# A RWKV-7 recurrence beside dense products: TensorE's order written out, preparation two chunks ahead, the inverse by blocks of 16, attention's parities in turn

## The chip, the cores and the metric

The kernel runs on one core of one Trainium2 chip. The metric is the device time of one execution in microseconds (us); the kernel before takes 3066.93 us, the median of three runs. Engines are TensorE (PE: matmuls; its weight loads, PEld, are listed apart), VectorE (DVE), ScalarE (ACT), GpSimd (POOL) and SyncE (SP, which issues the loads and stores).

## The reference

One inference step of a two-layer streaming encoder: 1024 new frames of one stream and 64 frames of another that is running. Width 1024, 16 heads of 64. Layer 0 mixes time by RWKV-7 and has a SwiGLU FFN; layer 1 is sliding-window attention with sinks over a shared key/value projection, and another FFN. All in float32. The recurrence, per head, with a 64×64 state:

```python
def step(s, inp):
    r_t, w_t, k_t, v_t, a_t, b_t = inp
    sa = jnp.einsum('bhvk,bhk->bhv', s, a_t)
    s = s * w_t[:, :, None, :] + sa[..., None] * b_t[:, :, None, :] + v_t[..., None] * k_t[:, :, None, :]
    return s, jnp.einsum('bhvk,bhk->bhv', s, r_t)
```

Its outputs are normalised per head, get a bonus term and a gate, and go through the output projection. Outputs of the whole are both streams' results, the two final states, the shift rows and the new key/value caches.

## The kernel before

**Dense products.** Weights are loaded in rows of 128×512 (`wr`), split into a high part `wh` (L393, ACT) and a remainder `wl` (L394, DVE or POOL); activations likewise into `xh` and `xl`. A product is three matmuls, `wh·xh`, `wh·xl`, `wl·xh` (L433, L434, L435), into a PSUM tile `dp`. Tokens go in two halves: A, of 512 columns (chunks 0 to 7), and B, of 576 (chunks 8 to 15 and the second stream), in pieces of 288 or 290 columns.

**Recurrence.** 17 chunks of 64 tokens: 0 to 7, 8 to 15, and 16, the second stream. A chunk is a few bursts of small matmuls between element-wise work:

- `prep` loads r, k, a and the decay; norms of the keys (`pn`, 8 matmuls, L106 to L117), scaled pairs `AR` and `BK`, the products G = BK·AR (two halves of 8 matmuls, into two banks of tag `rp` each, read out by L152 under a mask), and the bonus (L157, L158).
- `prep2` inverts the 64×64 triangular matrices of the 16 heads (`inverse`) and transposes BK into `BT` (L175 to L177). The inverse solves the four 32×32 diagonal quarters of all heads by substitution on DVE (15 steps, two columns a step, up to two parts each: L215 multiplies, L219 sums), after ACT has copied the triangles into a broadcast layout (L190), and joins quarters by two rounds of 16 matmuls of 32×32 (`r_ixd`, tag `rc`).
- `chain` is what follows from chunk to chunk: `U0` from the state M, `Up` = W·U0, the new state `Sp`, and the output Y of two state reads (even heads, then odd, kept in this order by a small memset `by`, L281) and the rows of G.
- `post` normalises (L318, L322 and L323 on POOL), transposes back (4 matmuls, `c_id` times `r_yc`), applies gate and bonus and stores z.

**Order.** Every instruction carries a priority (`Two`: one for TensorE, another for the rest), and a scheduler orders each engine's queue by it and by when operands will be there. Chunk i+1's `prep` and `prep2` stand behind chunk i's chain. The first eight chunks lie beside half B's decay, rate and gate stages and its v, r and k products; chunks 8 to 16 beside half A's output projection (`mix_out`), its norm, and the FFN of half A. An engine executes its queue in order and waits at an instruction whose semaphores aren't there yet.

**Attention.** For each pair of heads `attend` scales the probabilities, transposes them (`pt`, L1290), copies them out and multiplies by the values (`po`, L1294), first the one parity (partitions 0 to 63 of `po`) and then the other (64 to 127).

Of the kernel before, what the change touches and what calls it, by code (L numbers as in the profile page):

```python
# [9 lines left out]
F32 = mybir.dt.float32  # L10
F32R = mybir.dt.float32r
AF = mybir.ActivationFunctionType
ALU = mybir.AluOpType
# [34 lines left out]

class Rwkv:
# [32 lines left out]
    def start(self):  # L82

        nc = self.nc
        self.W = self.sb.tile([128, 8, 64], F32, name="W", tag="W", bufs=1)
        nc.gpsimd.memset(self.W, 0.0)

    def prep(self, ch):
# [14 lines left out]

        pn = self.pp()[0:64, 0:16].rearrange("p (par j) -> p par j", par=2)
        for j in range(8):
            self.mm(pn[:, :, j], lhsT=sq[:, j, :], rhs=c["bd"][:, 0:128:64], start=True, stop=True)  # L106
        n4 = self.t([128, 32], "n4")
        for q in range(4):
            d = 32 * (q % 2)
            V.tensor_scalar(out=n4[32 * q:32 * q + 32].rearrange("p (g j) -> p g j", g=4),  # L110
                            in0=mid(pn[d:d + 32, q // 2, :], 4), scalar1=1e-24, scalar2=None, op0=ALU.max)
        V.reciprocal(out=n4, in_=n4)
        nl = self.t([128, 32], "nl", 3)
        V.transpose(out=nl, in_=n4)

# [25 lines left out]


        X = self.t([128, 16, 128], "G", 2)
        flat2 = lambda x: x.rearrange("p a b -> p (a b)")
        for g in range(2):
            ps = [self.pp().rearrange("p (a b) -> p a b", a=4) for _ in range(2)]
            for i in range(4):
                for par in range(2):
                    h = slice(64 * par, 64 * par + 64)
                    self.mm(ps[par][:, i, :], lhsT=flat2(BK[h, 4 * g + i]), rhs=flat2(AR[h, 4 * g + i]), start=True, stop=True)  # L150
            for par in range(2):
                V.tensor_tensor(out=X[:, 8 * par + 4 * g:8 * par + 4 * g + 4, :], in0=ps[par], in1=mid(c["mask"], 4), op=ALU.mult)  # L152

# [5 lines left out]
        return dict(AR=AR, BK=BK, X=X, PC=PC, vf=vf, nl=nl)  # L159

    def prep2(self, d):
        nc = self.nc
        V, S = nc.vector, nc.scalar
        AR, X = d["AR"], d["X"]
        d["W"] = self.inverse(X, d["nl"])

        Xh = X.rearrange("p (par j) t -> p j par t", par=2)
        V.tensor_copy(Xh[0:64, :, 0, 0:64], AR[0:64, :, 0, :])
        S.copy(Xh[0:64, :, 1, 0:64], AR[64:128, :, 0, :])
        flat2 = lambda x: x.rearrange("p a b -> p (a b)")  # L170

        BT = d["BT"] = self.t([128, 16, 64], "BT")
        for g in range(2):
            ps = self.pp()
            for i in range(4):  # L175
                self.tr(ps[:, 128 * i:128 * i + 128], flat2(d["BK"][:, 4 * g + i]), self.c["id"])
            S.copy(flat2(BT[:, 8 * g:8 * g + 8, :]), ps)  # L177

    def inverse(self, X, nl):
# [4 lines left out]
        W = self.W  # L184
        Xh = X.rearrange("p (par j) t -> p j par t", par=2)
        st = self.t([128, 1024], "f4", 2)
        for q in range(4):
            d = 32 * (q % 2)
            src = Xh[d:d + 32, :, q // 2, d:d + 32].rearrange("p j t -> p t j").unsqueeze(2).broadcast_to([32, 32, 4, 8])
            S.copy(st[32 * q:32 * q + 32].rearrange("p (t g j) -> p t g j", g=4, j=8), src)  # L190
        N12 = self.t([128, 8, 32], "in12")
        S.copy(N12[0:32], Xh[0:32, :, 0, 32:64])
        S.copy(N12[64:96], Xh[0:32, :, 1, 32:64])
        NL = self.t([128, 1024], "f4", 2)
        V.transpose(out=NL, in_=st)
        NL = NL.rearrange("p (a b) -> p a b", a=32)
        V.tensor_tensor(out=NL, in0=NL, in1=mid(nl, 32), op=ALU.mult)

        one = NL.rearrange("p a b -> p (a b)")[:, 32:1024:66]
        ev = NL.rearrange("p (a two) b -> p a two b", two=2)  # L200

        Z = self.t([128, 1024], "f4", 2).rearrange("p (h c r b) -> p h c r b", h=2, c=4, r=4)
        tm = Z.rearrange("p h c r b -> p (h c r b)")[:, 0:512].rearrange("p (a b) -> p a b", b=32)
        V.tensor_tensor(out=tm, in0=bc(one, 32), in1=ev[:, :, 0, :], op=ALU.mult)
        V.tensor_tensor(out=ev[:, :, 1, :], in0=ev[:, :, 1, :], in1=tm, op=ALU.add)
        for i in (0, 3):
            V.tensor_tensor(out=Z[:, :, i], in0=c["xl0"].rearrange("p (h a b) -> p h a b", h=2, a=4),
                            in1=nl.unsqueeze(1).unsqueeze(1).broadcast_to([128, 2, 4, 32]), op=ALU.mult)
        for j in range(30, 0, -2):

            a, b = (0, 3) if j % 4 else (3, 0)
            part = [(h, (j // 4 + 1 - h) // 2) for h in range(2) if (j // 4 + 1 - h) // 2 < 4]
            for h, r0 in part:
                n = 4 - r0
                V.tensor_tensor(out=Z[:, h, 1:3, r0:4, 0:j],  # L215
                                in0=Z[:, h, a, r0:4, j:j + 2].rearrange("p r c -> p c r").unsqueeze(3).broadcast_to([128, 2, n, j]),
                                in1=NL[:, j:j + 2, 0:j].unsqueeze(2).broadcast_to([128, 2, n, j]), op=ALU.mult)
            for h, r0 in part:
                V.tensor_reduce(out=Z[:, h, b, r0:4, 0:j], in_=Z[:, h, min(a, 1):min(a, 1) + 3, r0:4, 0:j].rearrange("p c r j -> p r j c"),  # L219
                                axis=AX.X, op=ALU.add)  # L220
        XL = Z[:, :, 0]
        q4 = lambda x: x.rearrange("p h r (q f) -> p h (r q) f", f=4)[:, :, :, 0:2]
        V.tensor_copy(q4(XL), q4(Z[:, :, 3]))
        xe = XL.rearrange("p h r (a two) -> p h r a two", two=2)
        tm = Z[:, :, 1, :, 0:16]
        V.tensor_tensor(out=tm, in0=xe[:, :, :, :, 1], in1=one.unsqueeze(1).unsqueeze(1).broadcast_to([128, 2, 4, 16]), op=ALU.mult)  # L226
        V.tensor_tensor(out=xe[:, :, :, :, 0], in0=xe[:, :, :, :, 0], in1=tm, op=ALU.add)
        D3 = self.t([128, 3, 8, 32], "ixd")
        XD, WD, QT = D3[:, 0], D3[:, 1], D3[:, 2]
        for h in range(2):  # L230
            XO = Z[:, h, 1].rearrange("p a b -> p (a b)")
            V.transpose(out=XO, in_=XL[:, h].rearrange("p a b -> p (a b)"))
        for h in range(2):
            XO = Z[:, h, 1].rearrange("p a b -> p (a b)").rearrange("p (r g j) -> p j r g", r=4, g=4)
            V.tensor_copy(WD.rearrange("p j (r h g) -> p h j r g", r=4, h=2)[:, h], XO)
        V.transpose(out=XD.rearrange("p a b -> p (a b)"), in_=WD.rearrange("p a b -> p (a b)"))
        for q in range(4):
            f = (q % 2) * 32
            e = V.tensor_copy if q % 2 else S.copy
            e(W[32 * q:32 * q + 32, :, f:f + 32], WD[32 * q:32 * q + 32])  # L240
        ps = self.pc()[:, 0:256].rearrange("p (a b) -> p a b", a=8)
        for j in range(8):
            for lo in (0, 64):
                self.mm(ps[lo + 32:lo + 64, j, :], lhsT=N12[lo:lo + 32, j, :], rhs=XD[lo:lo + 32, j, :],
                                 start=True, stop=True)
        S.copy(QT[32:64], ps[32:64])
        V.tensor_copy(QT[96:128], ps[96:128])
        ps = self.pc()[:, 0:256].rearrange("p (a b) -> p a b", a=8)
# [6 lines left out]
        return W  # L255

    def chain(self, ch, d, M):
# [10 lines left out]
        Y, U0p = E(self.p([128, 512], "ry", 1)), E(self.pc())  # L268
        X, BT, W = d["X"], d["BT"], d["W"]
        heads = [(i, i // 2, slice(64 * (i % 2), 64 * (i % 2) + 64)) for i in range(16)]  # L270
        for i, j, h in heads:
            self.mm(U0p[h, j, :], lhsT=X[:, 8 * (i % 2) + j, 0:64], rhs=sv[:, i, :], start=True, stop=True)


        out = lambda j, par: Y[64 * (j % 2):64 * (j % 2) + 64, j // 2 * 2 + par, :]
# [6 lines left out]
        U0 = self.t([128, 8, 64], "yc")  # L282
        S.copy(U0, U0p)
        Up = E(self.pc())
        for i, j, h in heads:
            self.mm(Up[h, j, :], lhsT=W[h, j, :], rhs=U0[h, j, :], start=True, stop=True)
        V.tensor_copy(svh[0:64, :, 0, :], Up[0:64])
        S.copy(svh[0:64, :, 1, :], Up[64:128])
        Sp = E(self.pc())
        for i, j, h in heads:  # L290
            self.mm(Sp[h, j, :], lhsT=BT[:, i, :], rhs=sv[:, i, :], start=True, stop=True)

# [7 lines left out]
        Mn = self.t([128, 8, 64], "M", 2)  # L300
        V.tensor_tensor(out=Mn, in0=Sp, in1=M, op=ALU.add)
        V.tensor_tensor(out=Mn, in0=Mn, in1=bc(d["PC"], 64), op=ALU.mult)
        return Mn, Y

    def post(self, ch, d, Y):
        nc, c = self.nc, self.c
# [266 lines left out]
def tile_stream_step(ctx: ExitStack, tc: tile.TileContext, I, O):  # L573
# [439 lines left out]
    for n in ("tri", "mask", "bd", "xl0"):  # L1013
        const(n)
# [409 lines left out]
```

## Time and profile before

| | |
|---|---|
| Time, median of 3 runs | 3066.93 us (3064.41 to 3069.12) |
| Profiled execution | 3068.17 us, its span 3066.4 us |
| Mean granted clock of TensorE | 0.960 |
| ACT busy | 1371.4 us (45%) |
| POOL busy | 915.9 us (30%) |
| Main DMA queue | 285.81 MB, 31.3% of 16 engines |

The page lists each engine's busy time, cuts the span into 40 slices, and follows the chain of work that ended last; on that chain TensorE's dense products stand far ahead of all else. Other views group instructions by line and tile, list the waits of an engine by what released it, give busy time by windows, or show every instruction on a timeline. A small matmul of the recurrence leaves two records, so 16 matmuls show as x32.

### The profile page before, as it was taken

What the parts mean: (1) busy time and instruction counts of PE and PEld (TensorE: products, weight loads), DVE (VectorE), ACT (ScalarE), POOL (GpSimd) and SP (SyncE); (2) the same over time, 40 slices, a digit from 0 to 9 for tenths busy, and PEclk for the clock granted to TensorE, in tenths of its full rate; (3) what the DMA queues carried; (4) which work ended last, traced back from release to release, by engine and by line L of the source; (5) the groups of instructions that cost most, each with busy time, mean ns of one, the idle gap of its engine ahead of it and who ended that gap; (6) DMA issues with size and microseconds to landing.
All of it is one profiled execution on the core that took longest, in us unless ns stands there. A gap on an engine that the chain in (4) does not pass through costs nothing. (4 is left out here: it accounts for less than half of the span.)

```text
span 3066.4 us, 51529 instructions
## 1 busy us (share of the span) xinstructions
PE 2881.6 (94%) x19650; PEld 2475.1 (81%) x19650; DVE 1899.9 (62%) x3964; ACT 1371.4 (45%) x2489; POOL 915.9 (30%) x785
## 2 busy tenths in 40 slices
PE   6898888987999989999999999999999999999998
PEld 5677777876777767887789999887667889899998
DVE  8887798968998993357553333665555334633334
ACT  7766665544445542244653222344553233322222
POOL 6455123323343332224211222243111222322221
PEclk9999789989899999999999999999999999999999
DMA  4645353353232225232112222222112332322222
GB/s 144 174 119 149 109 140 102 109 130 118 77 97 87 90 70 139 93 111 86 62 42 73 83 83 83 77 82 79 59 62 67 95 96 73 110 83 83 84 82 70
DMA packets 262047, 289.10 MB, mean 94 GB/s; under 512 B 125028, under 2 KB 143972, under 8 KB 261800
## 3 DMA queue, kind: packets, MB, share of 16 engines
q1 hardware_dynamic: 261800, 285.81, 31.3%
q8 instruction: 154, 2.52, 0.4%
q14 instruction: 93, 0.76, 0.1%
HBM read 243.18 MB, written 41.16 MB: 93 GB/s over the span
## 5 line engine op out<-in xcount | busy, mean ns | idle before, releaser
L433 PE MATMUL dp<-xh,wh 128*128 128x288 f32 (+2 forms) x3480 | 1181.1, 341 | 26.1 <-DVE hx L962 10.2
L434 PE MATMUL dp<-xl,wh 128*128 128x288 f32 (+2 forms) x3480 | 1175.5, 338 | 10.6 <-POOL xl L426 6.3
L435 PE MATMUL dp<-xh,wl 128*128 128x288 f32 (+2 forms) x3480 | 1172.4, 337 | 0.0
L393 ACT CAST wh<-wr 128x512 fp32r<-128x512 f32 x730 | 446.2, 619 | 823.6 <-PE dp L434 633.0
L433 PEld LDWEIGHTS dp<-xh,wh 128*128 128x128 f32 x3480 | 667.0, 192 | 100.4 <-DVE hx L962 14.7
L434 PEld LDWEIGHTS dp<-xl,wh 128*128 128x128 f32 x3480 | 668.5, 192 | 73.3 <-POOL xl L426 7.6
L435 PEld LDWEIGHTS dp<-xh,wl 128*128 128x128 f32 x3480 | 668.7, 192 | 62.0 <-issue 6.2
L394 POOL TENSOR_TENSOR wl<-wr,wh 128x512 fp32r<-128x512 f32 x243 | 339.2, 1396 | 1059.0 <-ACT wh L393 954.0
L394 DVE TENSOR_TENSOR wl<-wr,wh 128x512 fp32r<-128x512 f32 x487 | 376.3, 776 | 431.5 <-ACT wh L393 423.0
L433 PE MATMUL dp<-mh,wh 128*128 128x288 f32 (+1 forms) x808 | 254.5, 315 | 1.2 <-DVE a_xB L962 1.0
L435 PE MATMUL dp<-mh,wl 128*128 128x288 f32 (+1 forms) x808 | 254.1, 314 | 0.0
L434 PE MATMUL dp<-ml,wh 128*128 128x288 f32 (+1 forms) x808 | 253.5, 314 | 0.0
L943 DVE TENSOR_TENSOR st<-st,dp 128x288 f32<-128x288 f32 (+1 forms) x132 | 70.0, 530 | 229.0 <-PE dp L435 228.6
L962 DVE TENSOR_TENSOR a_xB<-dp,a_xB 128x288 f32<-128x288 f32 x352 | 158.1, 455 | 82.9 <-PE dp L435 82.7
L945 POOL TENSOR_TENSOR xl<-st,xh 128x288 fp32r<-128x288 f32 (+1 forms) x102 | 101.8, 998 | 330.4 <-ACT xh L944 321.6
L433 PEld LDWEIGHTS dp<-mh,wh 128*128 128x128 f32 x808 | 152.3, 189 | 10.8 <-issue 2.4
L435 PEld LDWEIGHTS dp<-mh,wl 128*128 128x128 f32 x808 | 152.3, 188 | 8.1 <-issue 1.8
L434 PEld LDWEIGHTS dp<-ml,wh 128*128 128x128 f32 x808 | 152.4, 189 | 6.6 <-issue 0.8
L190 ACT COPY r_f<-r_G 32x1024 f32<-32x1024 f32 x68 | 136.0, 1999 | 37.1 <-DVE r_f L226 25.0
L962 DVE TENSOR_TENSOR hx<-dp,hx 128x512 f32<-128x512 f32 x176 | 119.5, 684 | 44.9 <-PE dp L435 44.4
L215 DVE TENSOR_TENSOR r_f<-r_f,r_f 128x60 f32<-128x60 f32 (+5 forms) x476 | 119.2, 281 | 0.5
L944 ACT CAST xh<-st 128x288 fp32r<-128x288 f32 (+1 forms) x102 | 50.2, 492 | 136.2 <-DVE st L943 135.1
(343 smaller groups left out, 3889.3 us busy)
## 6 DMA issues: line engine op xcount, KB each, us to landing
wr<-in_ffn_in SPq DMA_DIRECT2D x352, 256.0 KB
wr<-in_ffn_out SPq DMA_DIRECT2D x176, 256.0 KB
wr<-in_rkv SPq DMA_DIRECT2D x90, 256.0 KB
wr<-in_rwo SPq DMA_DIRECT2D x32, 256.0 KB
wr<-in_wq SPq DMA_DIRECT2D x32, 256.0 KB
wr<-in_wo SPq DMA_DIRECT2D x32, 256.0 KB
r_r_s<-s_s SPq DMA_DIRECT2D x17, 256.0 KB
r_sv<-s_vt SPq DMA_DIRECT2D x17, 256.0 KB
```

The lines of the kernel that those rows point to most:

```text
L190: S.copy(st[32 * q:32 * q + 32].rearrange("p (t g j) -> p t g j", g=4, j=8), src)
L215: V.tensor_tensor(out=Z[:, h, 1:3, r0:4, 0:j], in0=Z[:, h, a, r0:4, j:j + 2].rearrange("p r c -> p c r").unsqueeze(3).broadcast_to([128, 2 ...
L393: nc.scalar.copy(h, x)
L394: (nc.gpsimd if self.turn % 3 == 0 else nc.vector).tensor_tensor(out=l, in0=x, in1=h, op=ALU.subtract)
L433: self.nc.tensor.matmul(ps, lhsT=wh, rhs=xh, start=i == 0, stop=False)
L434: self.nc.tensor.matmul(ps, lhsT=wh, rhs=xl, start=False, stop=False)
L435: self.nc.tensor.matmul(ps, lhsT=wl, rhs=xh, start=False, stop=i == last)
L943: V.tensor_tensor(out=t[o], in0=t[o], in1=p, op=ALU.mult)
L944: S.copy(a.hi[:, q], t[o])
L945: G.tensor_tensor(out=a.lo[:, q], in0=t[o], in1=a.hi[:, q], op=ALU.subtract)
L962: V.tensor_tensor(out=self.x[m][:, q], in0=p, in1=self.x[m][:, q], op=ALU.add)
```

## The change

A class `Pump` opens a region in which TensorE's queue is taken in the order in which the code issues it; the other engines keep the scheduler. `recur` becomes a generator: between two bursts it yields how many ns of dense work shall come first, and `Dense.mm` counts them off after each triple, at 0.44 ns a column and 6 a triple.

```diff
+    def tick(self, n):
+        if self.gen is None:
+            return
+        self.need -= 0.44 * n + 6
+        while self.gen is not None and self.need <= 0:
+            self.step()
...
+            if self.pump:
+                self.pump.tick(3 * ps.shape[1])
```

A chunk's wants are 2, 2, 1, 1, 1, 1 us between the bursts of the chain and the transposes of the chunk before it, 3, 0, 1 us around the preparation of the chunk after next, 1.5, 2.5, 1.5 us between the rounds of the next chunk's inverse, and then 2 us (4 in the second stretch): 19.5 or 21.5 us.

```diff
+        for i, ch in enumerate(chunks):
+            k = rw.chain(ch, ds[i], M)
+            step(k, base)
+            yield 2 * us
+            step(k, base)
+            yield 2 * us
+            step(k, base)
...
+            if i + 2 < len(chunks):
+                yield from prep(i + 2, inv)
             if i + 1 < len(chunks):
+                for want in (1.5, 2.5, 1.5, 0):
+                    step(vs[i + 1], inv)
+                    yield want * us
+            if i + 2 < len(chunks):
+                inverse(i + 2, inv)
+            yield free * us
+        step(old, fill)
...
     all(rkv("B", "k", xs["Bk"]))
+    pump.drain()
```

Whatever steps are left when half B's k product ends, the drain issues one behind the other. Chunks 8 to 16 become one run of the generator, beside the same dense work as before.

The inverse solves 16×16 blocks. The matrices of all heads are laid out so that the two 16-blocks of a quarter sit in the lanes of one tile (`e` holds 0/1 masks of lanes), the tiles `f4` go from 128×1024 to 128×512, ACT's broadcast copies from 1024 to 512 elements, and the substitution has 7 steps of one multiplication and one sum:

```diff
-        for j in range(30, 0, -2):
+        for j in range(14, 0, -2):
...
-            for h, r0 in part:
-                n = 4 - r0
-                V.tensor_tensor(out=Z[:, h, 1:3, r0:4, 0:j],
...
+            r0, n = j // 2, 8 - j // 2
+            V.tensor_tensor(out=Z[:, 1:3, r0:8, 0:j],
...
+        for j in range(8):
+            for q in range(4):
+                o = slice(32 * q, 32 * q + 32)
+                self.mm(ps[o, j, :], lhsT=T(q, j, slice(o.start % 64, o.start % 64 + 32)), rhs=XD[o, j, 0:16], start=True, stop=True)
+        S.copy(Q1[:, :, 0:16], ps)
+        yield
...
+                self.mm(ps[o, j, :], lhsT=Q1[o, j, :], rhs=WD[o, j, 16:32], start=True, stop=True)
+        V.tensor_tensor(out=WD[:, :, 16:32], in0=ps, in1=WD[:, :, 16:32], op=ALU.add)
+        turn()
```

Two rounds of 32 matmuls join the 16-blocks to quarters; the two rounds of 16 that join quarters stay. The constant `xl0` is built on the chip instead of loaded, `BT` gets two buffers, and U0 another tile.

In attention both parities are transposed and copied before the products, which then run by segment, the parities in turn:

```diff
-                for si, (at, n, vv) in enumerate(seg):
+                eTs.append(eT)
+
+            for si, (at, n, vv) in enumerate(seg):
+                for par, eT in enumerate(eTs):
```

Of the 128 `po` matmuls on TensorE's queue, 32 pairs of neighbours had different parity, and now 45 do.

**TensorE's queue inside a chunk.** A piece of it before, in the first stretch (lines L433 to L435 are dense; `r_AR,r_BK` is G, `r_ixd,r_in` the first old round of the inverse, `c_id,r_yc` the output transposes, `r_rkr,c_bd` the bonus):

```order
L433 MATMUL dp_6649<-xh_6249,wh_6611 128x290
L73 MATMUL p_rp_4139<-r_AR_4113,r_BK_4114 128x128 x4
L73 MATMUL p_rc_4025<-r_ixd_4015,r_in_192_3945 32x32 x8
L77 MATMUL p_ry_3825<-c_id,r_yc_3926 128x128 x4
L73 MATMUL p_rc_4025<-r_ixd_4015,r_in_192_3945 32x32 x8
L73 MATMUL p_rp_4152<-r_rkr_4116,c_bd 128x512
L434 MATMUL dp_6649<-xl_6250,wh_6611 128x290
L435 MATMUL dp_6649<-xh_6249,wl_6612 128x290
L433 MATMUL dp_6649<-xh_6256,wh_6617 128x290
```

After, in the second stretch (L113 and L117 issue the recurrence's matmuls, L521 to L523 are dense): the end of G's second half, the bonus, and the two BK transposes.

```order
L113 MATMUL p_rp_7918<-r_AR_7711,r_BK_7712 128x128
L113 MATMUL p_rp_7919<-r_AR_7711,r_BK_7712 128x128
L521 MATMUL dp_7892<-xh_7753,wh_7886 128x512
L522 MATMUL dp_7892<-xl_7754,wh_7886 128x512
L523 MATMUL dp_7892<-xh_7753,wl_7887 128x512
L113 MATMUL p_rp_7935<-r_rkr_7714,c_bd 128x512
L117 MATMUL p_rp_7939<-c_id,r_BK_7712 128x128 x4
L117 MATMUL p_rp_7945<-c_id,r_BK_7712 128x128 x4
L521 MATMUL dp_7892<-xh_7760,wh_7886 128x512
L522 MATMUL dp_7892<-xl_7761,wh_7886 128x512
```

Before, bursts of several steps came close together, inside a dense triple where they fell; now they stand between whole triples, at the places that the wants give them, and G's two parities alternate.

**TensorE's queue at the end of half B's products.** Before, in the last dense triples (`r_BT` is Sp, `r_G` the rows of Y, `c_bd,r_rt` the key norms of chunk 8):

```order
L433 MATMUL dp_7421<-xh_6909,wh_7389 128x290
L73 MATMUL p_rc_5133<-r_sv_5080,r_BT_5067 64x64
L73 MATMUL p_ry_5084<-r_sv_5080,r_G_4793 64x64 x2
L434 MATMUL dp_7421<-xl_6910,wh_7389 128x290
L73 MATMUL p_rc_5133<-r_sv_5080,r_BT_5067 64x64 x15
L73 MATMUL p_ry_5084<-r_sv_5080,r_G_4793 64x64 x14
L435 MATMUL dp_7421<-xh_6909,wl_7390 128x290
L73 MATMUL p_rp_7461<-c_bd,r_rt_7458 64x2 x8
L77 MATMUL p_ry_5084<-c_id,r_yc_5185 128x128 x4
L73 MATMUL p_rp_7497<-r_AR_7484,r_BK_7485 128x128 x4
L73 MATMUL p_rp_7498<-r_AR_7484,r_BK_7485 128x128 x4
L73 MATMUL p_ry_7745<-r_M_5174,r_AR_7484 64x64 x8
```

After (`r_iqt` is the last round of chunk 7's inverse, `r_rt,W` is Up; the last rows begin the output projection):

```order
L113 MATMUL p_rc_7527<-r_ixd_7250,r_in_339_7220 32x32
L113 MATMUL p_rc_7548<-r_ixd_7250,r_iqt_7526 32x32 x16
L113 MATMUL p_rc_7571<-r_sv_7567,r_G_6993 64x64 x16
L113 MATMUL p_rc_7590<-r_rt_7588,W 64x64 x16
L113 MATMUL p_rc_7609<-r_sv_7567,r_BT_7029 64x64 x16
L117 MATMUL p_ry_7405<-c_id,r_yc_7448 128x128 x4
L113 MATMUL p_ry_7636<-r_M_7380,r_AR_6837 64x64 x16
L113 MATMUL p_ry_7636<-r_sv_7567,r_G_6993 64x64 x16
L117 MATMUL p_ry_7636<-c_id,r_yc_7679 128x128 x4
L521 MATMUL dp_7791<-xh_7725,wh_7779 128x512
L522 MATMUL dp_7791<-xl_7726,wh_7779 128x512
```

Chunk 7's chain had dense triples between its bursts and chunk 8's preparation behind it; now no dense triple stands between its steps, and chunk 8's preparation comes behind the first dense triples of the output projection.

**DVE's queue in the inverse.** Before, the first of the substitution's steps, two parts each:

```order
L215 TENSOR_TENSOR r_f_68_2949<-r_f_68_2949,r_f_67_2946 128x2x30
L215 TENSOR_TENSOR r_f_68_2949<-r_f_68_2949,r_f_67_2946 128x2x26
L219 TENSOR_REDUCE r_f_68_2949<-r_f_68_2949 128x30
L219 TENSOR_REDUCE r_f_68_2949<-r_f_68_2949 128x26
L215 TENSOR_TENSOR r_f_68_2949<-r_f_68_2949,r_f_67_2946 128x2x28
L215 TENSOR_TENSOR r_f_68_2949<-r_f_68_2949,r_f_67_2946 128x2x24
L219 TENSOR_REDUCE r_f_68_2949<-r_f_68_2949 128x28
L254 COPY W<-p_rc_2708 32x8x32
L219 TENSOR_REDUCE r_f_68_2949<-r_f_68_2949 128x24
```

After, nearly all of them:

```order
L268 TENSOR_TENSOR r_f_65_3479<-r_f_65_3479,r_f_64_3475 128x2x14
L271 TENSOR_REDUCE r_f_65_3479<-r_f_65_3479 128x14
L268 TENSOR_TENSOR r_f_65_3479<-r_f_65_3479,r_f_64_3475 128x2x2x12
L271 TENSOR_REDUCE r_f_65_3479<-r_f_65_3479 128x2x12
L268 TENSOR_TENSOR r_f_65_3479<-r_f_65_3479,r_f_64_3475 128x2x3x10
L271 TENSOR_REDUCE r_f_65_3479<-r_f_65_3479 128x3x10
L268 TENSOR_TENSOR r_f_65_3479<-r_f_65_3479,r_f_64_3475 128x2x4x8
L271 TENSOR_REDUCE r_f_65_3479<-r_f_65_3479 128x4x8
L268 TENSOR_TENSOR r_f_65_3479<-r_f_65_3479,r_f_64_3475 128x2x5x6
L271 TENSOR_REDUCE r_f_65_3479<-r_f_65_3479 128x5x6
L268 TENSOR_TENSOR r_f_65_3479<-r_f_65_3479,r_f_64_3475 128x2x6x4
L271 TENSOR_REDUCE r_f_65_3479<-r_f_65_3479 128x6x4
```

28 multiplications and 28 sums became 7 and 7.

More of the change, by code (lines that the diff above doesn't have):

```diff
@@ L46, in __exit__, with __init__, start, end @@
         return False
+class Pump:
+    def __init__(self, tc):
+        self.tc, self.gen, self.need, self.region = tc, None, 0.0, None
+    def start(self, gen, priority):
+        self.gen, self.need, self.prio = gen, 0.0, int(priority * 1000000)
+        if self.region is None:
+            self.region = self.tc.manual_schedule(engines={mybir.EngineType.PE})
+            self.region.__enter__()
+        self.tick(0)
+    def end(self):
+        self.region.__exit__(None, None, None)
+        self.region = None
+    def tick(self, n):
[4 more added lines that the diff above has]
+            self.step()
+    def step(self):
+        outer, self.tc.cur_priority = self.tc.cur_priority, self.prio
+        want = next(self.gen, None)
+        self.prio, self.tc.cur_priority = self.tc.cur_priority, outer
+        if want is None:
+            self.gen = None
+        else:
+            self.need += want
+    def drain(self):
+        while self.gen is not None:
+            self.step()
 class Rwkv:
@@ L102, in prep @@
         S.activation(sq, kkr, AF.Square)
[L104 to L114, printed above, removed]
         IP, P = s, self.tmp(65)
@@ L193, in inverse @@
[L193 to L203, printed above, removed]
@@ L221, in inverse @@
[L221 to L228, printed above, removed]
@@ L229, in inverse @@
[L229 to L236, printed above, removed]
@@ L281, in chain @@
         by = G.memset(self.t([1, 1], "by", 2), 0.0)
[L282 to L291, printed above, removed]
+        yield
         odd = seen(1)
@@ L356, in __init__ @@
         self.n = self.turn = 0
-        self.more = self.esb = None
+        self.more = self.esb = self.pump = None
         self.mixed = []
@@ L1053, in tile_stream_step @@
+    pump = dn.pump = Pump(tc)
+    pump.start(recur(range(8), M, 1, 2, FREE[0], {7: lambda M: state.append(M)}), 1)
+    state = []
     prio(2)
@@ L1074, in tile_stream_step @@
     F = Ffn("A", 0, xA, x0)
-    all(F.main())
+    for _ in F.main():
+        if pump.region and not pump.gen:
+            pump.end()
     rctx.close()
```

257 lines of the change are left out of this document (183 added, 74 removed).

## The prediction

> **What bounds the kernel now.** I read the page first, engines and slices:
>
> ```profile
> span 3066.4 us, 51529 instructions
> ## 1 busy us (share of the span) xinstructions
> PE 2881.6 (94%) x19650; PEld 2475.1 (81%) x19650; DVE 1899.9 (62%) x3964; ACT 1371.4 (45%) x2489; POOL 915.9 (30%) x785
> ...
> PEclk9999789989899999999999999999999999999999
> ```
>
> TensorE is busy 94% of the span, so whatever leaves its time as it is cannot help. Its granted clock (last row, tenths) is below 9 only in the early slices, where the recurrence runs. So I cut that part, 270 to 1190 us, at the end of the r/k/v products of half B (661) and at the resumption of full dense flow (702). Columns: length, busy PE, weight loads, DVE, ACT, POOL, then clock, DMA share, GB/s.
>
> ```profile
> 270.00:661.00 391.00, 346.69 (x3571) 306.27 (x3571) 321.00 (x898) 238.03 (x378) 123.40 (x104) 0.88 0.43 119
> 661.00:702.00 41.00, 26.97 (x141) 20.82 (x141) 26.10 (x40) 19.86 (x26) 14.82 (x13) 0.67 0.59 142
> 702.00:1190.00 488.00, 443.93 (x3652) 345.67 (x3651) 425.02 (x1076) 232.29 (x324) 170.07 (x134) 0.92 0.29 89
> ```
>
> PE idles 44 + 14 + 44 = 102 us here, and DVE is busy 82% and 87% of the two long stretches: nowhere else is it so near TensorE. The dense products alone (same windows, tile `dp`; first number PE), and two stretches of pure dense flow later in the program:
>
> ```profile
> 270.00:661.00 391.00, 226.02 (x1287) 193.11 (x1287) 0.00 (x0) 47.43 (x112) 0.88 0.43 119
> 702.00:1190.00 488.00, 325.63 (x1188) 233.99 (x1186) 47.94 (x71) 9.77 (x17) 0.92 0.29 89
> 2387.00:2464.00 77.00, 77.00 (x332) 62.10 (x331) 27.02 (x40) 22.68 (x38) 17.88 (x14) 1.00 0.31 95
> 2695.00:2772.00 77.00, 77.00 (x580) 77.00 (x580) 28.39 (x56) 21.10 (x41) 17.15 (x16) 1.00 0.27 84
> ```
>
> Undisturbed, a 512-column product costs 77/332 = 0.232 us and a 288-column one 77/580 = 0.133. The first stretch holds 1287 of about 290 columns, 171 us; the second 1188 of 512, 276 us. What is left over is the price of the recurrence on TensorE: 391 − 171 = 220 us for eight chunks, **27.5 us each**, and 488 − 276 = 212 us for nine, **23.6 us each**. The question is what this becomes.
>
> What PE waits for (us in total, times, longest; the last three from 702 to 1190, the first from 270 to 661, the second between):
>
> ```profile
> PE p_rc L73 <- ACT r_ixd L246: 10.1, 4, 4.3
> PE p_rp L73 <- ACT r_rt L102: 8.8, 1, 8.8
> PE p_rc L73 <- DVE r_ixd L236: 5.9, 3, 3.4
> PE p_rc L73 <- DVE r_ixd L247: 5.9, 3, 3.0
> PE p_rc L73 <- DVE W L254: 3.6, 2, 2.4
> ```
>
> Waits are few, and when they come they last some 2 us: the inverse's handoffs (`r_ixd`, `W`). Usually dense fills the time. There is a second loss, the clock:
>
> ```profile
> 1018.42 0.39 PE L435 MATMUL dp<-xh,wl 128*128 128x512 f32 x1
> 1020.36 0.68 PE L73 MATMUL p_ry<-r_M,r_AR 64*64 64x64 f32 x16 [1.55 <-POOL r_by L281]
> 1021.47 1.07 PE L73 MATMUL p_rc<-r_ixd,r_in 32*32 32x32 f32 x32 [0.42 <-DVE r_ixd L236]
> ...
> 1023.05 0.63 PE L434 MATMUL dp<-xl,wh 128*128 128x512 f32 x1
> 1023.48 0.63 PE L435 MATMUL dp<-xh,wl 128*128 128x512 f32 x1
> ...
> 1021.30:1028.00 6.70, 6.54 (x45) 5.31 (x46) 5.80 (x8) 6.62 (x8) 2.33 (x3) 0.50 0.17 51
> ```
>
> After idle of 1.55 and 0.42 us around two small bursts, dense products start 0.43 us apart instead of 0.23, and the window's clock is 0.50. Clock short of 1 is 0.12 × 391 + 0.08 × 488 = 86 us; some of it falls on idle. I estimate 60 us lost to it, 3.5 a chunk.
>
> **The change, part by part.** TensorE's own bursts for one chunk (timeline; start, duration; a matmul leaves two records):
>
> ```profile
> 642.06 0.66 PE L77 MATMUL p_ry<-c_id,r_yc 128*128 128x128 f32 x4
> 653.58 1.14 PE L73 MATMUL p_rc<-r_yc,W 64*64 64x64 f32 x30
> 658.87 1.09 PE L73 MATMUL p_rc<-r_sv,r_BT 128*64 128x64 f32 x29
> 659.80 1.03 PE L73 MATMUL p_ry<-r_sv,r_G 128*64 128x64 f32 x27
> 708.76 1.16 PE L73 MATMUL p_rp<-r_AR,r_BK 64*128 64x128 f32 x16
> 772.55 1.09 PE L73 MATMUL p_rp<-c_bd,r_rt 128*64 128x2 f32 x16 [0.38 <-ACT r_BT L177]
> 1031.24 1.15 PE L73 MATMUL p_rc<-r_sv,r_G 128*64 128x64 f32 x32
> 1032.32 0.69 PE L73 MATMUL p_rc<-r_ixd 32*32 32x32 f32 x30
> ```
>
> What the order keeps: U0 1.15, Up 1.15, Sp 1.09, the two state reads 2 × 0.68, the G rows 1.03, output transposes 0.66, norms 1.09, G 2 × 1.16, the bonus (two records of 512 columns) 0.46, BK transposes 2 × 0.66, the two old inverse rounds 1.07 + 0.74: 13.4 us. G comes in alternating halves now, as at 708.76, so this price holds for all chunks.
>
> *Added:* two rounds of 32 matmuls 32×16, 64 records each. From below, a round costs what 16 of the old do (0.93, at 32 records); from above twice the 1.07 row. So 1.9 to 4.3 us a chunk; I take 2.8, nearer the cheap end because 16 columns are half of 32. Over 17 chunks 32 to 73 us, 48 taken. Own time: **16.2 us**.
>
> *Removed from DVE and ACT:*
>
> ```profile
> L215 DVE TENSOR_TENSOR r_f<-r_f,r_f x476: 128/206/1448, 311.6 to 1140.0; 128x48 f32<-128x48 f32 x34, 128x60 f32<-128x60 f32 x18, 128x72 f32<-128x72 f32 x18, 128x64 f32<-128x64 f32 x12
> L219 DVE TENSOR_REDUCE r_f<-r_f x476: 152/238/306, 312.5 to 1140.7; 128x24 f32<-128x72 f32 x34, 128x30 f32<-128x90 f32 x18, 128x36 f32<-128x108 f32 x18, 128x32 f32<-128x96 f32 x12
> sum 920.00, DVE 330.21 ACT 135.96; mean DVE 110.07 ACT 45.32
> L152 DVE TENSOR_TENSOR r_G<-p_rp,c_mask 128x512 f32<-128x512 f32 x68 | 45.8, 682 | 12.7 <-PE p_rp L73 12.1
> ```
>
> Substitution goes from 28 pairs to 7: at the medians 206 and 238 ns, 12.4 us to 3.1. All work on tile `r_f` (third row) is 330/17 = 19.4 us a chunk; the remaining 7.0 are whole-tile operations, whose tiles halve. About 13 us a chunk leave DVE, 220 of its 772 in these stretches, and ACT's broadcast copies (136/17 = 8.0) halve. None of that is on the path by itself, since dense covers it; it is worth what it makes of the waits.
>
> *The fixed order:* the scheduler no longer puts dense before a late recurrence step; everything behind a late step waits, 19.5 or 21.5 us of dense per chunk included, and with it the weight tiles' release to ACT, POOL and SP's loads. Where is a step late although the code leaves room? The second half of G follows the first with no dense between and needs its banks read by two evictions of 0.68 (fourth row): 1.4 us. The bonus and the BK transposes share those two banks: 1.8. Ten other handoffs have 1 to 3 us of dense ahead and one or two evictions of 0.4 to 0.7 us: 0.2 each, 2.0. Sum 5.2. From below nothing; from above the 2 us of the waits quoted at each of the ten, 20 more.
>
> *The clock:* the long idles go, but dense comes in pieces of 1 to 3 us between bursts. Between 0 and today's 3.5 a chunk; I take 1.0, since the fall shown needed idle next to bursts. The Trainium skill ("TensorE: Matmul & The Clock Gate", section "Why this matters for your kernels") says that only idle gaps of about 3 us bring the clock down. By that rule this term is 0, the sum 17 us lower; the trace, with 0.50 after 1.55 us, is against it.
>
> So a chunk costs 16.2 + 5.2 + 1.0 = **22.4 us**. First stretch: 8 × (27.5 − 22.4) = −41. Second: 9 × (23.6 − 22.4) = −11, but the norm behind the A half's output projection has no recurrence between its rows now, and the preamble for chunks 8 and 9 starts later:
>
> ```profile
> 756.00:771.00 15.00, 3.71 (x10) 2.28 (x10) 0.69 (x1) 0.85 (x2) 0.66 0.22 72
> 670.00 1.86 PE L73 MATMUL p_rp<-c_bd,r_rt 128*64 128x2 f32 x16 [8.84 <-ACT r_rt L102]
> 684.54 1.65 PE L433 MATMUL dp<-xh,wh 128*128 128x512 f32 x3
> ```
>
> Dense fills 3.7 of those 15 us and recurrence about 6 more, which must now go elsewhere (+6); the later start I put at +4. Second stretch: −1. At the seam (661 to 702) half B's products now end before chunk 7's last steps, so its chain runs bare: about 23 us from the first inverse round to the output transposes, some 15 of them counted above; before, 8.84 us of idle and the cold preparation of chunk 8 lay there. I call it +2, within ±10.
>
> *Attention:* products of opposite parity that stand side by side overlap:
>
> ```profile
> 1524.05 1.22 PE L1294 MATMUL po<-a_PT,vtok 64*64 64x256 f32 x4
> 1534.95 0.65 PE L1294 MATMUL po<-a_PT,vtok 128*64 128x256 f32 x4
> ```
>
> Two matmuls (4 records) take 0.65 instead of 1.22. The order has 45 such neighbours instead of 32: 13 × 0.57 = 7.4 at most, 0 at least; I take −4.
>
> Sum: −41 − 1 + 2 − 4 = −44 us. The profiled execution took 3068.17 (span 3066.4 and 1.8 around it), 1.2 above the median 3066.93. So 3068 − 44 = 3024, on the median's scale **3023**.
>
> **Rivals.** *Slower: late steps stall a fixed order.* The mechanism is the one above: PE waits for the inverse's evictions with dense queued behind. The idle quoted there averages 2.0 us (5.9 in three). With two such a chunk stalls are 9.2 us, +68 us: **3091**. It decides from 5.2 + 44/17 = 7.8 us of stalls a chunk. For it: PE is in order, and DVE also runs the preparation and weight splits. Against it: DVE loses a third of its work per chunk, and preparation is two chunks ahead.
>
> *No gain: the added matmuls and the clock eat it.* With rounds at 4.3 (+26) and the clock at 2.5 a chunk (+26): about **3075**. For it: 64 short records a round, more pieces; against: the 0.74 price of the shortest old round.
>
> *The clock holds.* If idles under 2 us no longer bring it down once the long ones are gone, the clock term alone falls away: 3023 − 17 = **3006**. It stands inside the forecast's range and I give it 0.08 of that chance, for the 1.55 us idle above speaks against it. (The page named above would have it so.)
>
> *A larger gain.* DVE relieved, handoffs on time: stalls 3.2 (−34), clock 0 (−17): **2972**. For it: today's waits all name DVE or ACT, in stretches where DVE is over 80% busy. Against it: G's own 1.4 us and the shared banks remain.
>
> **Chances.** Forecast (2995 to 3055) 0.46, 0.08 of it the holding clock; larger gain 0.20; no gain 0.12; slower 0.22. A measurement here tells no change from about 0.2%, 6 us. Forecast and larger gain are faster, with a third of the no-gain case: 0.70; the same 0.08; slower 0.22. The range takes in the larger gain and the stalled order's price: 2962 to 3092.
>
> **What would show it.** Cut alike, the changed profile should show PE's overhead per chunk near 22 us in both stretches; tile `r_f` on DVE near 7 us a chunk; clock at 0.95 or more; waits of PE under `p_rp` (G) before those under `p_rc`; the two new rounds under 1.5 us each. PE idle under `p_rc` or `W` of over 8 us a chunk would be the stalled order, and a clock still at 0.9 the no-gain case. A long bare stretch at the seam, well over 40 us, would break the third term.

## The result and the profile after

The changed kernel takes **3109.92 us** (median of four runs, 3108.75 to 3111.73) against 3065.67 us before: ratio 1.0143, 95% interval 1.0126 to 1.0161, **slower by 1.4%**. The forecast was 3023 us, range 2962 to 3092. The profiled execution spans 3107.8 us, 41.4 more than before.

First the page of the changed kernel: busy time by engine, and the clock by slices.

```profile
PE 2859.6 (92%) x21826; PEld 2456.5 (79%) x21826; DVE 1758.5 (57%) x3326; ACT 1306.7 (42%) x2471; POOL 900.3 (29%) x786
...
PEclk9999879997899999999999999999999999999999
```

DVE lost 141 us of work and ACT 65, the direction that the change was made for, and the program became slower: TensorE's busy time fell by 22 us (2881.6 to 2859.6) while the span grew by 41, so its idle time grew by 63. The same cut as before the change, at the places where the work stands now (half B's last product ends at 681, just ahead of the cut at 684; the output projection begins at 728), first all work, then tile `dp` alone, then the sum for tile `r_f` from 270 to 1190, then all work of the 60 us behind:

```profile
270.00:684.00 414.00, 347.36 (x4262) 301.21 (x4262) 266.99 (x579) 205.46 (x367) 116.87 (x99) 0.89 0.40 109
684.00:728.00 44.00, 17.62 (x392) 14.96 (x390) 19.11 (x32) 7.84 (x15) 15.86 (x14) 0.55 0.36 111
728.00:1190.00 462.00, 392.09 (x4660) 297.71 (x4661) 339.14 (x724) 195.83 (x301) 148.97 (x129) 0.92 0.30 88
...
270.00:684.00 414.00, 235.35 (x1336) 199.91 (x1334) 0.00 (x0) 48.19 (x115) 0.89 0.40 109
684.00:728.00 44.00, 0.00 (x0) 0.00 (x0) 0.00 (x0) 0.00 (x0) 0.55 0.36 111
728.00:1190.00 462.00, 262.09 (x934) 177.65 (x935) 35.52 (x52) 7.41 (x13) 0.92 0.30 88
...
sum 920.00, DVE 160.15 ACT 73.25; mean DVE 53.38 ACT 24.42
...
1190.00:1250.00 60.00, 60.00 (x261) 48.73 (x260) 23.44 (x33) 17.20 (x29) 13.32 (x11) 1.00 0.56 142
```

At 0.133 us for a product of half B and 0.232 for one of 512 columns, the first stretch holds 1336 × 0.133 = 178 us of dense work and leaves 236 (220 before); the last holds 934 × 0.232 = 217 and leaves 245 for nine chunks, 27.2 each (212 and 23.6 before); between them no dense product runs for 47 us (681.2 to 728.4). `r_f` on DVE did fall, from 330 to 160 us, and the clock did not rise: 0.89 and 0.92, against 0.88 and 0.92. About 60 us of dense work that the kernel before had done by 1190 are still to do; there PE is busy without a gap.

Where the 41 us come from, by the same dense product in both traces: half B's last ends at 681.2 instead of 661.2 (+20); the output projection begins at 728.36 instead of 684.54, so the seam (the time between these two products) adds 24; by the end of the recurrence it is +65, so the last stretch adds another 21; in attention 22 are made up, and about 3 behind it. What PE waits for, from 270 to 1250 us of the changed kernel (total, times, longest):

```profile
PE p_rp L113 <- DVE r_G L212: 33.0, 18, 4.0
PE p_rc L113 <- DVE r_ixd L289: 18.2, 9, 6.3
PE p_rp L117 <- ACT r_BT L228: 17.2, 6, 5.1
PE dp L521 <- ACT xh L513: 15.9, 4, 7.5
PE p_rp L117 <- DVE r_vf L221: 14.4, 11, 3.3
PE p_ry L113 <- DVE r_g L414: 11.3, 12, 1.8
PE p_ry L117 <- POOL r_yc L409: 10.5, 2, 7.4
PE p_rc L113 <- ACT r_sv L359: 8.8, 9, 1.9
```

The first row is the second half of G, which waits for the banks of the first, in nearly every chunk. The third and fifth are the second BK transpose, which waits for a bank that the bonus or the first transpose holds. One such place on the timeline (start, duration, idle before):

```profile
608.78 1.16 PE L113 MATMUL p_rp<-r_AR,r_BK 64*128 64x128 f32 x16
611.50 1.75 PE L113 MATMUL p_rp<-r_AR,r_BK 64*128 64x128 f32 x16 [1.55 <-DVE r_G L212]
613.18 0.61 PE L521 MATMUL dp<-xh,wh 128*128 128x290 f32 x1
...
614.31 0.44 PE L522 MATMUL dp<-xl,wh 128*128 128x290 f32 x1
614.55 0.45 PE L523 MATMUL dp<-xh,wl 128*128 128x290 f32 x1
```

The wait is 1.55 us, the second half takes 1.75 instead of 1.16, and the dense products behind it start 0.24 us apart instead of 0.133: the granted clock is 1.00 up to 613.1 and 0.50 from 613.2 to 616.5. What the wait costs is more than its length here.

### The profile page after: what moved, and what is told of

It reads as the page before. It is cut to its first block, busy times and chain, and to the rows that moved or that the text cites. A ratio compares the mean times of both kernels' runs of the same rounds, so it can differ in the third digit from the quotient of the medians.

```text
span 3107.8 us, 55302 instructions
## 1 busy us (share of the span) xinstructions
PE 2859.6 (92%) x21826; PEld 2456.5 (79%) x21826; DVE 1758.5 (57%) x3326; ACT 1306.7 (42%) x2471; POOL 900.3 (29%) x786
## 5 line engine op out<-in xcount | busy, mean ns | idle before, releaser
L521 PE MATMUL dp<-xh,wh 128*128 128x288 f32 (+2 forms) x3480 | 1194.0, 344 | 36.8 <-ACT xh L513 22.3
L523 PE MATMUL dp<-xh,wl 128*128 128x288 f32 (+2 forms) x3480 | 1164.4, 335 | 0.0
L521 PEld LDWEIGHTS dp<-xh,wh 128*128 128x128 f32 x3480 | 667.3, 192 | 118.5 <-ACT xh L513 25.7
L523 PEld LDWEIGHTS dp<-xh,wl 128*128 128x128 f32 x3480 | 668.4, 192 | 55.9 <-issue 2.1
L482 POOL TENSOR_TENSOR wl<-wr,wh 128x512 fp32r<-128x512 f32 x243 | 332.1, 1367 | 1158.7 <-ACT wh L481 1031.1
L521 PE MATMUL dp<-mh,wh 128*128 128x288 f32 (+1 forms) x808 | 254.5, 315 | 0.3 <-DVE hx L1052 0.2
L523 PE MATMUL dp<-mh,wl 128*128 128x288 f32 (+1 forms) x808 | 254.0, 314 | 0.0
L521 PEld LDWEIGHTS dp<-mh,wh 128*128 128x128 f32 x808 | 152.5, 189 | 10.7 <-issue 3.0
L523 PEld LDWEIGHTS dp<-mh,wl 128*128 128x128 f32 x808 | 152.6, 189 | 8.5 <-issue 2.4
L245 ACT COPY r_f<-r_G 32x512 f32<-32x512 f32 x68 | 73.2, 1077 | 79.5 <-DVE r_G L212 78.8
L1031 ACT ACTIVATE st<-dp 128x288 f32<-128x288 f32 (+1 forms) x132 | 62.2, 471 | 93.1 <-PE dp L523 92.8
```

The lines of the kernel that those rows point to most:

```text
L245: S.copy(st[32 * q:32 * q + 32].rearrange("p (t e g j) -> p t e g j", t=16, e=2, g=2), src)
L482: (nc.gpsimd if self.turn % 3 == 0 else nc.vector).tensor_tensor(out=l, in0=x, in1=h, op=ALU.subtract)
L521: self.nc.tensor.matmul(ps, lhsT=wh, rhs=xh, start=i == 0, stop=False)
L523: self.nc.tensor.matmul(ps, lhsT=wl, rhs=xh, start=False, stop=i == last)
L1031: S.activation(t[o], p, AF.Silu)
```

## The experiments

Times stand against runs of the kernel before on the same chip. Where a run is set against the changed kernel, that is its 3109.92 us from another session; the medians of the kernel before lie between 3065.3 and 3068.7 us in all of them.

**Attention alone.** The kernel before with the loops of the change's last diff.

> The kernel before with the change's attention part alone. Theory A (the two traces: from the start to the end of attention the changed kernel makes up about 24 us there, 65 us behind before it and 40 after): about 24 us faster than before, 3042 us, and as many po products overlapped in pairs as in the changed kernel. Rival: the 24 us come from elsewhere (other weights in flight, a different phase of the queues), and the part alone gives the 4 us of the prediction, 3062.

Measured: 3043.92 us against 3065.3, ratio 0.9943 (0.9924 to 0.9961): **21 us faster**, Theory A. In the changed kernel an overlapped pair reads as the rows below, two matmuls (four records) in 0.65 us; one after the other two take 1.22. Counted in the traces (the second matmul's first record starts 0.01 us behind the first's), 45 pairs (of 64 that the 128 matmuls could form) overlap in this run and in the changed kernel, 16 in the kernel before:

```profile
1542.80 0.65 PE L1447 MATMUL po<-a_PT,vtok 64*64 64x256 f32 x4
1549.79 0.65 PE L1447 MATMUL po<-a_PT,vtok 64*64 64x256 f32 x4
```

**Transposes first, products one parity after the other.** The loops of the run before, with the inner two exchanged:

```diff
-            for si, (at, n, vv) in enumerate(seg):
-                for par, eT in enumerate(eTs):
+            for par, eT in enumerate(eTs):
+                for si, (at, n, vv) in enumerate(seg):
```

> The kernel before with attention's transposes of both parities ahead of the products, but the products still one parity after the other. Theory A (neighbours of different parity overlap, that is the gain): nearly all of the gain is gone, within 6 us of before. Rival: the gain comes from taking the transposes out of the way (fewer waits for the copies): 15 to 24 us faster than before.

Measured: 3063.63 us, ratio 0.9995 (0.9979 to 1.001), and 16 overlapped pairs as before. No gain clear of the noise is left: it is the alternation.

**The recurrence's part alone.** The changed kernel with attention as before.

> The changed kernel with attention as before the change: the recurrence's part alone. Theory (the parts add; the attention part alone gave 21 us): 3110 + 21 = about 3131 us, 65 us slower than before. Rival (the two parts share a cost, such as the weights' loads behind them): 3110 to 3120.

Measured: 3129.3 us against 3068.74, ratio 1.0209 (1.0173 to 1.0245): 61 us slower by the medians, 64 by the ratio. The parts add within the noise.

**The inverse by 16 alone,** in the scheduler's order and with preparation one chunk ahead.

> The kernel before (scheduler's order, preparation one chunk ahead) with the inverse by blocks of 16 alone. Theory A (the inverse takes load off DVE and its two added rounds cost 0.73 us each): 10 to 25 us faster than before, DVE's work on tile r_f about 160 us instead of 330. Rival (the added 64 short matmuls a chunk are what costs, 45 us or more in all): the same or slower, 3066 to 3100.

Measured: 3066.13 us, ratio 1.0007 (0.9997 to 1.0017): no difference. Theory A's gain did not come, and `r_f` on DVE fell to 185 us, not to 160; the rival's number came. From 270 to 1190 us, first this kernel and then the one before:

```profile
270.00:1190.00 920.00, 848.75 (x9509) 708.71 (x9508) 656.82 (x1361) 421.05 (x707) 301.92 (x251) 0.87 0.37 107
...
270.00:1190.00 920.00, 817.59 (x7361) 672.77 (x7362) 772.11 (x2012) 490.17 (x728) 308.29 (x251) 0.89 0.36 104
```

DVE has 115 us less and ACT 69 less to do; PE is busy 31 us longer, and idle as much less. So PE waits 31 us less, as a relief of DVE and ACT would have it (that it is the relief isn't tested by itself); longer work on PE (the added rounds, at a clock of 0.87 instead of 0.89) takes as much back.

**The same code without the fixed order.** `Pump` doesn't open its region; the scheduler orders TensorE too.

```diff
-            self.region = self.tc.manual_schedule(engines={mybir.EngineType.PE})
-            self.region.__enter__()
+            self.region = True
```

> The changed kernel without the fixed order on TensorE: the same code in the same sequence, but the scheduler orders TensorE's queue too, by priority and readiness. Theory A (PE's waits for a late step, 63 us of idle before recurrence bursts in the second stretch against 37 before, and the bare seam are the loss): 3110 falls to about 3040 or below, idle before the recurrence's bursts near that of before. Rival (preparation two chunks ahead or the inverse is at fault, not the order): stays above 3090.

Measured: 3163.66 us, ratio 1.0331 (1.0302 to 1.036): slower still. This theory fell as it was put: giving the order back to the scheduler doesn't cure it. The rival's number came, but the run can't say whether the early preparation or the inverse would be at fault. With the low priorities that the steps carry, dense work runs ahead and the recurrence is left nearly bare in two long stretches at low clock (tile `dp` has PE busy 22 of the 197 us and 90 of the 283):

```profile
556.00:753.00 197.00, 148.72 (x2247) 129.65 (x2245) 142.06 (x334) 70.44 (x114) 59.02 (x56) 0.65 0.28 81
1217.00:1500.00 283.00, 216.46 (x2858) 187.90 (x2859) 182.12 (x386) 94.65 (x155) 74.97 (x67) 0.73 0.28 79
```

The run says nothing of a scheduler with other priorities. So I asked what the order lacks.

**Dense work between G's halves.**

```diff
             step(g, p)
-            yield 3 * us
+            yield 1.5 * us
             step(g, p)
+            yield 1.5 * us
             step(g, p)
```

> The changed kernel, with 1.5 us of dense work between the two halves of G, taken from the 3 us ahead of them. In the changed kernel PE waits 33.0 us in 18 times at the second half for the read of the first (two reads of 0.68 us). Theory B (a fixed order costs where it leaves no cover): that wait falls below 10 us, the time from 3110 to about 3088. Rival (DVE comes late to these reads whatever stands between): over 20 us remain, 3100 to 3110.

Measured: 3075.7 us, ratio 1.003 (1.0017 to 1.0043): **34 us faster than the changed kernel**, more than expected, though the wait stayed above the 10 us of the theory. The largest waits of this kernel, and its last stretch:

```profile
PE dp L521 <- ACT xh L513: 16.0, 5, 7.2
PE p_rp L117 <- DVE r_vf L221: 15.5, 16, 1.4
PE p_rc L113 <- DVE r_ixd L289: 14.6, 11, 4.3
PE p_rp L113 <- DVE r_G L212: 12.7, 18, 2.2
...
716.00:1190.00 474.00, 420.73 (x4809) 318.93 (x4809) 344.80 (x743) 204.73 (x317) 159.19 (x135) 0.95 0.34 99
```

G's wait fell from 33.0 to 12.7, 20 us. It wasn't alone: the second BK transpose's wait for `r_BT` fell from 17.2 to 2.9, and a wait of the inverse for `Q` rose from 0.4 to 7.1. In all, PE idles 226 us of this program instead of 248 and is busy 2850 instead of 2860: of the 31 us between the two profiled executions, 22 are idle and 9 busy time. The clock of the last stretch rose from 0.92 to 0.95.

**The bonus step at the inverse's priority** (`step(g, p)` instead of `step(g, fill)` there).

> The changed kernel, with the step of the bonus and the BK transposes issued at the priority of the inverse instead of the lower one for filling. In the changed kernel PE waits 31.6 us at the second BK transpose, for the bonus's read on DVE and the first transpose's on ACT, which stand behind the inverse's work on these engines. Theory B (PE's new waits are read-outs that are queued late behind other work): these waits fall to about 12 us, the time from 3110 to about 3092. Rival (the step is late for its own length, two read-outs of 0.6 us, or the time only moves to the next wait): waits as before or moved, 3105 to 3115.

Measured: 3097.96 us, ratio 1.0102 (1.0083 to 1.0122): 12 us faster than the changed kernel, less than expected, and not by the path expected. The waits for `r_vf` and `r_BT`, 31.6 us in all, became 22.5 and 2.3, where about 12 were expected: the bonus's read stays late. Theory B holds in sign.

**The first stretch's wants times 0.9.**

```diff
-            self.need += want
+            self.need += want * (0.9 if self.prio < 3000000 else 1.0)
```

> The changed kernel, with every want of dense work in the first stretch times 0.9, so that chunk 7's steps up to its output transposes stand beside half B's products instead of behind them. Theory C (the bare chain at the seam costs: 44 us without a dense product in the changed kernel, 23.5 before): the stretch without dense falls to about 25 us and the time from 3110 to about 3090. Rival (the chain's latency is only moved, and closer bursts stall as much more): within 6 us of 3110.

Measured: 3103.56 us, ratio 1.0126 (1.0108 to 1.0143): 6 us. The stretch without dense work did shrink, from 47 to 20 us (dense ends at 696.3, begins again at 716.3), but half B's products end 15 us later, since PE must do the same bursts among them. PE's idle time in the seam fell by 9 us only, from 28 to 19: most of what went was work that had to be done elsewhere. The rival is nearer.

**All three.**

> The changed kernel with all three edits: the bonus step's priority, dense between G's halves, wants of the first stretch times 0.9. Theories B and C: their gains add, 3110 - 18 - 22 - 20 = about 3050, idle of PE before recurrence bursts near that of the kernel before. Rival (the time is the sum of what PE must do, and a stall removed here comes back at the next handoff): 3085 or more.

Measured: 3070.54 us, ratio 1.0017 (1.0002 to 1.0031), between the two: 39 us of the 60 expected. The gains (34, 12, 6) sum to 52.

**More cover at the handoffs that still wait.** Beside the first two of those edits, and with the first stretch's wants times 0.8 instead of 0.9 (the main lines; the expectation below names the rest):

```diff
-            self.need += want
+            self.need += want * (0.8 if self.prio < 3000000 else 1.0)
...
+            if g == 0:
+                d["vf"] = vf
+                yield
...
-            yield 2 * us
+            yield 2.75 * us
...
-                for want in (1.5, 2.5, 1.5, 0):
+                for want in (2, 3, 1.5, 0):
...
-FREE = (2.0, 4.0)
+FREE = (0.5, 1.5)
```

> The changed kernel with the three edits of the run before, and with the wants of dense work laid where PE still waits there (1 us between the two BK transposes, 0.75 more ahead of Sp and of the even state read, 0.5 more ahead of the second and third round of the inverse, taken from the want at a chunk's end; first stretch times 0.8 so that chunk 7 is covered). Theory B (what a fixed order costs is cover missing at single handoffs): from 3070 to about 3050, idle before recurrence bursts from 84 to about 50 us. Rival (the remainder is the seam, the stages and dense work's own waits, or stalls move on): 3065 to 3075.

Measured: 3046.72 us against 3066.78, ratio 0.994 (0.9923 to 0.9957): 63 us faster than the changed kernel, 20 faster than the one before. The last stretch and the largest waits:

```profile
687.00:1190.00 503.00, 455.57 (x4943) 347.60 (x4944) 363.21 (x766) 219.70 (x339) 172.47 (x146) 0.95 0.35 103
...
PE p_ry L117 <- POOL r_yc L411: 12.7, 2, 6.5
PE dp L523 <- ACT xh L515: 11.5, 5, 5.0
PE p_rp L113 <- DVE r_G L212: 10.4, 15, 2.0
```

Not all of this is cover at handoffs inside a chunk. Against the run with three edits it is 24 us faster, and 16 of them stand already where the output projection begins: at 687.3 instead of 703.2 us, 2 us behind half B's last product (685.3). Chunk 7's chain is covered now, and the bare stretch at the seam is gone.

**The kernel before without chunks 0 to 7.**

> The kernel before without the recurrence of chunks 0 to 7: their z is filled with zeros, and chunk 8 starts from a zero state. It measures what the first stretch costs without them. Theory D (27.5 us a chunk in the prediction held other work too: half B's decay, rate and gate stages, whose short products and waits cost about 37 us beyond the 171 of dense columns): from 270 us to the end of half B's products takes 171 + 37 = about 208 us. Rival (those waits are there only because the recurrence holds ACT and DVE): about 175 us.

Measured: 2869.36 us, a single run. All work, and tile `dp`, of the first stretch:

```profile
270.00:485.00 215.00, 195.61 (x1270) 179.97 (x1269) 55.28 (x68) 102.43 (x213) 39.99 (x27) 0.91 0.61 161
...
270.00:485.00 215.00, 195.61 (x1270) 179.97 (x1269) 0.00 (x0) 46.08 (x109) 0.91 0.61 161
```

Half B's products end at 485 us: 215 us from 270 with no recurrence at all, where 171 were counted as dense. Theory D holds: 44 us of the first stretch belong to the stages (the short products of decay, rate and gate) and to dense work's own waits. A chunk there costs (391 − 215)/8 = 22.0 us.

## Why the prediction was wrong, point by point

Taken by the same dense products in both traces, the first stretch moved by +20 us where −41 was forecast, the seam by +24 (+2), the last stretch by +21 (−1), and attention by −22 (−4).

**The step that failed first: "27.5 us each".** The prediction took what was left of the first stretch, 220 us, as "the price of the recurrence on TensorE". Without the eight chunks 44 of it are still there. At 22.0 us a chunk, a changed chunk of 22.4 has nothing to win: the −41, nearly the whole forecast, was other work divided by the number of chunks. (With the same 44 us taken off, a chunk of the changed kernel costs about (411 − 178 − 44)/8 = 23.6 there, and chunk 7's chain has moved out of that stretch into the seam.) The nine chunks of the last stretch read 23.6 us, where few short stages run; that the two disagreed by 4 us was the sign.

**The chunk's price was too low: 22.4 forecast, 27.2 measured** in the last stretch. (Against 23.6 before, part of this is where the windows begin: the one at 702 leaves some of chunk 8's preparation ahead of it, the one at 728 doesn't. By the same dense products the stretch is 21 us longer, 2.3 a chunk.)

- *The added rounds* (2.8 us) were priced too high, if anything: an uncovered one reads 0.73 us at full clock, so 1.5 a chunk. The 1.07 us row, behind the upper bound and in the sum of 13.4, stands in the window whose clock was 0.50; the same round takes 0.69 at full clock (950.42 in the rows further down).

```profile
686.00 0.73 PE L113 MATMUL p_rc<-r_ixd,Q 32*32 32x16 f32 x64 [0.38 <-ACT Q L303]
```

- *Stalls* (5.2): G was put at 1.4 us and reads 33.0/17 = 1.9; bonus and BK transposes at 1.8 and read 31.6/17 = 1.9. All rows of the recurrence in the wait view (the eight above show most) sum to 124 us, about 20 of them at the seam: some 6.1 a chunk. Places and sizes were nearly right.
- *The clock* (1.0) was wrong. I let it recover because "the long idles go" and the fall shown "needed idle next to bursts". The granted clock of the last stretch is 0.92 before and after; 0.08 × 462 us is 37 us or 4.1 a chunk, part of it on idle. And a fall doesn't need a wait. In the kernel before, bursts stand close together from 948.4 to 953 us, with PE busy 4.31 of 4.60 us, and behind them the clock is 0.51 and dense products start 0.43 us apart:

```profile
948.36 1.09 PE L73 MATMUL p_rc<-r_sv,r_BT 128*64 128x64 f32 x29
949.29 1.03 PE L73 MATMUL p_ry<-r_sv,r_G 128*64 128x64 f32 x27
950.42 0.69 PE L73 MATMUL p_rc<-r_ixd,r_in 32*32 32x32 f32 x32
951.31 1.09 PE L73 MATMUL p_rp<-c_bd,r_rt 128*64 128x2 f32 x16 [0.19 <-ACT r_BT L177]
952.33 1.45 PE L73 MATMUL p_rp<-r_AR,r_BK 64*128 64x128 f32 x8
...
954.30 0.63 PE L434 MATMUL dp<-xl,wh 128*128 128x512 f32 x1
954.73 0.63 PE L435 MATMUL dp<-xh,wl 128*128 128x512 f32 x1
...
946.00:953.00 7.00, 6.71 (x127) 5.53 (x126) 6.65 (x18) 2.69 (x6) 1.41 (x2) 1.00 0.40 115
953.00:956.40 3.40, 3.40 (x11) 2.63 (x10) 3.08 (x11) 3.31 (x6) 0.00 (x0) 0.51 0.00 0
```

So the going of long idles was no reason for the clock to recover. Dense work between G's halves shortened waits and raised the clock at once (0.92 to 0.95); the sum had them as two separate terms.

With these sizes, 14.5 us of own work, 6.1 of stalls and 4.1 of clock make about 25 of the 27.2; this is an estimate, since part of the clock's loss falls on idle.

**The norm and later preamble** (+10 in the last stretch, 1.1 a chunk) were not tried by themselves; they are inside the 27.2.

**The seam** was +2 within ±10; it added 24, and the sign that the prediction named, a bare stretch well over 40 us, came with 47. The bare chain was foreseen, its end was not: the two longest waits, 7.42 us for POOL in `post` and 7.48 for the split of z, stand behind it, and chunk 8's preparation, which before filled that time, comes later.

```profile
719.76 1.11 PE L117 MATMUL p_ry<-c_id,r_yc 128*128 128x128 f32 x4 [7.42 <-POOL r_yc L409]
728.36 0.79 PE L521 MATMUL dp<-xh,wh 128*128 128x512 f32 x1 [7.48 <-ACT xh L513]
```

**Attention** was the right mechanism, its size off by a factor of five: −4 forecast, −21 measured. I counted neighbours in the order, 13 more, at 0.57 us. In the traces 29 more pairs overlap, 45 instead of 16, which at that price is 16.5 of the 21 us; what makes the rest is not shown. The 45 of the new order was right; of the 32 neighbours in the old order only 16 overlapped when they ran, and why is not shown. I should have counted overlapped pairs in the trace.

**The rivals.** The slower one named the kind of loss, a fixed order that waits for late steps, and its side. It put it at the inverse's evictions and at 3091; the largest waits are at G and the BK transposes, those under `p_rc` are some 2 us a chunk instead of the 8 that were its sign, and the seam comes on top. "No gain" had a part too: in the run with the inverse alone PE idles 31 us less and works 31 us longer. With cover in the right places (3046.72) the fixed order is about even with the scheduler's, 3043.92 for the kernel before with attention's part alone; about 21 us of the gain of either are attention's. The run at 3046.72 keeps the early preparation and the inverse by 16, so what the two cost together, cover can make up.

**Smaller readings.** `r_f` fell to 160/17 = 9.4 us a chunk, where near 7 was named as the sign, so DVE lost 10 us a chunk on it instead of 13. DVE is nearer to TensorE at the program's start than in the recurrence (66.5 against 52.6 us in the first 77), and not all of today's waits name DVE or ACT: the 1.55 us one in the prediction's rows names POOL.

What stays open: how much of the shorter busy time of G's split is the clock, why the bonus's read stays late at the higher priority, what preparation two chunks ahead is worth by itself (no run has it alone), and whether a fixed order with still better cover beats the scheduler's.

## What to carry to other kernels

Before a leftover is divided by a count, run the stretch without the thing that is counted: here 44 us belonged to others. Where an engine's order is written out, every handoff needs cover as long as its read-outs, two banks that are both read before both are written again above all; a wait view by releaser shows which lacks it, and work moved there from a place with slack can be worth more than the wait. When work moves from one engine to the one that bounds the kernel, price both sides there: here 31 us less idle met 31 us more busy time.

## What the runs showed of the hardware

- Bursts of small matmuls bring the clock down with short waits between them, or hardly any. After 1.55 us idle between two bursts of G, dense products start 0.24 us apart instead of 0.133, at a granted clock of 0.50. In the kernel before, the clock fell to 0.51 behind bursts that left 0.29 us idle in 4.60. The Trainium skill ("TensorE: Matmul & The Clock Gate", section "Why this matters for your kernels") puts the limit at idle gaps of about 3 us; these traces don't agree, the clock was down after half of that, and after less.
- Products that write different partition halves of one bank can overlap fully when they stand side by side: two in 0.65 us instead of 1.22. Over attention, 29 more such pairs were worth 16.5 of the 21 us gained.
